# A hybrid encoder block on one core: a wider in-projection chunk, a tap on another engine, a regrouped filter chain and regrouped attention products

## The chip, the cores and the metric

The kernel runs on one core of a Trainium2 chip. The metric is the device time of one execution in microseconds (us); of several runs the median counts. TensorE does the matrix products (PE in the rows; PEld is its loading of weights), VectorE (DVE) and ScalarE (ACT) the elementwise work, GpSimd (POOL) the rest of it, and SP issues most of the transfers.

## The reference

Inputs are x (1, 2048, 1024) in f32, p, and the weights of one layer. What matters here:

```python
h = rms_norm(x, g_mix);  proj = h @ w_in           # w_in: 1024 x 2304
q, k, v, u = proj[:512], proj[512:640], proj[640:768], proj[768:]   # last axis
ya = attention_group(q, k, v, q_gain, k_gain)      # 8 query heads, 2 kv heads, 64 each
yh = hyena_group(u, conv_w, conv_b, ...)           # 3 x 512 channels
x = x + concat(group_rms(ya), group_rms(yh)) @ w_out
x = x + hierarchical_moe(rms_norm(x))              # 32 experts, top 2 of one group
x = x + (p @ w_ple) * sigmoid(rms_norm(x) @ w_ple_gate + b)
return rms_norm(x)
# hyena_group: uc = conv_b + sum_j shift(u, j) * conv_w[j]  (3 taps), split into v, x1, x2
#   y = x2 * conv(h2, x1 * conv(h1, v)); the filters h1, h2 (2048 long, two-sided) come from
#   a small sine network times a decay, divided by the sum of their absolute values, by FFT
```

## The kernel before

The program is written as Python generators that emit instructions; a framework sets semaphores, assigns buffers from pools and orders each engine's queue when the program is built, earlier emitted work first where it can go. `block_kernel` (L1787) runs two generators side by side with `interleave` (L91): each yields the planned cost of what it has just emitted, and the one that is behind its share goes next.

The left side is `stage_in` (L104) and then `Attention.run` (L749). `stage_in` takes the tokens in four quarters of 512. A quarter normalises and transposes its x (L157 to L178) into a high and a low part, `xh` and `xl`. Then come three chunks of 256 columns of `w_in` for q, k and v (`tokens`, L181): a weight chunk is loaded (L133), split into high and low (`split_w`, L136: ScalarE copies the high part, GpSimd or VectorE subtracts), and `product` (L145) makes 24 matmuls for each of four token tiles, into one of three PSUM banks (`in_pm`, L114); ScalarE copies the result out (L187) and one store for each chunk sends it to `qkv_d`. Then twelve tiles of 128 channels for the Hyena inputs (`channels`, L192): a product with 512 tokens, a copy into `U` (L204), the three-tap convolution with the middle tap on VectorE (L209) and the two others after it (L212), four transposes back to token order (L219), a copy and stores to `uc_d`. In the last quarter the attention's pools open (L236), its first preparation (`begin`) is emitted between the channel tiles, and `K.uc_done` tells the right side which third of `uc_d` is complete.

The right side is `stage_filter` (L319), `stage_hyena` (L482), and part of the per-layer embedding (`Ple.run`, L1501). The filter stage makes a small sine network's output `h2`, and then takes eight pairs of order and channel block: `gen` (L384) in eight turns makes a product (L394), multiplies by the decay into `g` (L401, eight buffers, `GB`) and adds up absolute values (L402); `norm` (L407) sums (L411 to L422, each product through the one bank of `fi_p`), scales `g` (L435) and corrects one row (L437); `fft1` (L440) makes eight products (L444, the same bank), copied out by ScalarE (L446) and stored; `fft2` (L450) follows one pair later. L467 to L479 emit `gen` of one pair, `fft1` of the pair before and `fft2` of the one before that in turn. `stage_hyena` transforms `uc_d` blocks, multiplies with the filters and transforms back; L541 is the gating after its last product.

`Attention.run` goes through 16 units (8 heads, two halves of the queries). For each of 16 key tiles a unit makes four score products (L798, L801) into two `ps` banks, two exponentials on ScalarE (L802), and two value products (L811), which lag two key tiles behind (`PV_LAG`); GpSimd and VectorE add up the exponentials (L821). Each step also emits up to two steps of the next unit's preparation (L733, L735). `K.behind` keeps score and value products in order. The banks:

```python
banks = {"pa": [(psa, "pa")] * 3, "ps": [(pss, "ps")] * 2}
for j, (h, u) in enumerate(self.order):
    wait -= K.banks_free                 # set when the right side has emitted its last
    if wait == -BANKS_AFTER:             # BANKS_AFTER = 2
        psx = self.pool("at_px", 1, space=PSUM)
        for tag in banks:
            banks[tag].append((psx, tag))
```

After both sides come the output projection, the experts and the tail, which the change leaves alone.

Of the kernel before, what the change touches and what calls it, by code (L numbers as in the profile page):

```python
# [8 lines left out]
F32 = mybir.dt.float32  # L9
# [27 lines left out]
GB = 8  # L37
# [5 lines left out]
PV_LAG = 2  # L43
# [60 lines left out]
def stage_in(K, st, x, g_mix, w_in, conv_w, conv_b, qkv_d, uc_d, pa, attn):  # L104
# [9 lines left out]
    pst, psm = pool("in_pt", 2, s_ps, space=PSUM), pool("in_pm", 3, s_ps, space=PSUM)  # L114
# [6 lines left out]
    K.uc_done, K.banks_free = 0, False  # L121
# [9 lines left out]
    def load_w(c0, n, pool, tag):  # L131
        raw = pool.tile([P, 8, n], F32, tag=tag, name="raw")
        nc.sync.dma_start(raw, w_in[:, c0:c0 + n].rearrange("(k p) n -> p k n", p=P))  # L133
        return raw

    def split_w(raw, n, pool, tags, on_pool, bufs=2):  # L136
        wh, wl = [pool.tile([P, 8, n], F32R, tag=tag, name=nm, bufs=bufs) for tag, nm in zip(tags, ("wh", "wl"))]
# [5 lines left out]
        return wh, wl  # L143

# [7 lines left out]
    for h in range(NQ):  # L152
        last, first = h == NQ - 1, h > 0
        xh, xl = [[pa.tile([P, 4, HT], F32R, tag=f"{nm}{q}", name=nm) for q in range(2)] for nm in ("xh", "xl")]
        cols = [2, 0, 1] if last else [0, 1, 2]
        raws = []
        for t in range(HTT):  # L157
# [5 lines left out]
            if t < 2:  # L163
                raws.append(load_w(cols[t] * 256, 256, praw, "raw"))
# [16 lines left out]
        def tokens(c, wh, wl):  # L181

            stg = pa.tile([P, HTT, 256], F32, tag="stg", name="stg", bufs=2)
            for t in range(HTT):
                ps = psm.tile([P, 512], F32, tag="pm", name="ps")
                product(ps[:, :256], lambda k: xs(k, slice(t * P, (t + 1) * P)), lambda k: (wh[:, k], wl[:, k]))
                nc.scalar.copy(stg[:, t], ps[:, :256])  # L187
                yield 2.6
            nc.sync.dma_start(qkv_d[h * HT:(h + 1) * HT, c * 256:(c + 1) * 256]
                              .rearrange("(t p) n -> p t n", p=P), stg)  # L190

        def channels(ct, stg, wh, wl):  # L192
# [10 lines left out]
            product(ps, lambda k: (wh(k), wl(k)), lambda k: xs(k, slice(None)))  # L203
            nc.scalar.copy(U[:, o0:o0 + HT], ps)  # L204
            if not last:
# [3 lines left out]
            nc.vector.tensor_scalar(out=acc[:, :n_out], in0=U[:, 1:1 + n_out], scalar1=wcol(1),  # L209
                                    scalar2=wcol(3), op0=ALU.mult, op1=ALU.add)  # L210
# [3 lines left out]
            if first:  # L214
                nc.gpsimd.tensor_copy(fix[:, h - 1, ct:ct + 1], acc[:, 0:1])
            pt = pst.tile([P, 512], F32, tag="pt", name="pt")
            for k in range(HTT):
                t0 = o0 - 1 + k * P
# [8 lines left out]
        for c in cols:  # L227
            raw = raws.pop(0) if raws else load_w(c * 256, 256, praw, "raw")
            if h == 0 and c == 0:
                consts()  # L230
            yield from tokens(c, *split_w(raw, 256, pw, ("wh", "wl"), not (c == 2 or (h == 0 and c < 2))))
        if last:
            while not K.filter_done:
                yield 0.05
            s_e.close()
            pb = attn.open(lambda tag: pst.tile([P, 512], F32, tag="pt", name=tag))  # L236
            ahead = attn.begin()
            raws = [load_w(768 + i * P, P, pb, "raw") for i in range(2)]
        for ct in range(12):
            part, cs = ct // 4, slice(ct // 2 % 2 * 256, (ct // 2 % 2 + 1) * 256)  # L240
            if last:
                raw = raws.pop(0)
                w4 = split_w(raw, P, pb, ("w", "w"), ct % 3 != 2, 4)
                if ct < 10:
                    raws.append(load_w(768 + (ct + 2) * P, P, pb, "raw"))
                wh, wl = [lambda k, w=w: w[:, k] for w in w4]
            else:
                if ct % 2 == 0:
                    raw = load_w(768 + ct * P, 256, praw, "raw")
                    w4 = split_w(raw, 256, pw, ("wh", "wl"), ct % 6 != 4)  # L250
                wh, wl = [lambda k, w=w: w[:, k, ct % 2 * P:(ct % 2 + 1) * P] for w in w4]
# [1645 lines left out]
```

## Time and profile before

| | |
|---|---|
| median of 3 runs | 3165.42 us (3157.89 to 3170.35) |
| profiled execution, its own time | 3178.87 us |
| its span, first to last instruction | 3177.1 us |
| TensorE busy | 2905.4 us (91%) |
| VectorE, ScalarE, GpSimd busy | 2047.3, 1322.0, 1143.2 us |
| mean granted TensorE clock | 0.951 of full |
| instructions | 50424 |

Busy time is a sum over stages with different limits, so a view by stretch says more than the whole. A wait in a row is idle time of the engine named first, put down to what came last. An instruction's line is the line of the kernel that made it; one made by a helper carries the helper's line (L74, L80, L88). Matmuls overlap, so the distance from start to start tells their cost better than their duration.

### The profile page before, as it was taken

How to read it: one execution, taken by the hardware profiler on the slowest of the kernel's cores; microseconds unless marked ns; L12 is line 12 of the kernel's file. 1: busy time of each engine (PE TensorE's matmuls, PEld its weight loads, DVE VectorE, ACT ScalarE, POOL GpSimd, SP SyncE). 2: the span in 40 equal slices, each digit the busy share in tenths (PEclk: the TensorE clock that was granted, in tenths of full speed). 3: DMA queues.
4: the chain of work that ended last, by engine and by line, in shares of the span. 5: the costliest groups of instructions: out<-in, count | busy, mean ns of one | idle time of the engine just before them, and what ended most of it. 6: DMA issues, size and time to landing. Idle time of an engine off the chain costs nothing. (4 is left out here: it accounts for less than half of the span.)

```text
span 3177.1 us, 50424 instructions
## 1 busy us (share of the span) xinstructions
PE 2905.4 (91%) x19001; PEld 1937.3 (61%) x19001; DVE 2047.3 (64%) x2737; ACT 1322.0 (42%) x1975; POOL 1143.2 (36%) x1058
## 2 busy tenths in 40 slices
PE   7989889798899999759999999989999999998897
PEld 5757667575445453524444488856667777675776
DVE  5865656536677776628887745366667677675665
ACT  3232233332344434225444422245556566664332
POOL 1423323242355555218877643011111211121443
PEclk9989889898999999879999999989999999999999
DMA  6477787786755765651000254379789888897553
GB/s 196 146 219 245 212 251 238 225 262 187 222 164 171 204 179 168 177 170 44 18 12 15 65 168 140 137 230 337 249 274 340 292 305 284 309 322 250 180 180 112
DMA packets 471989, 627.45 MB, mean 197 GB/s; under 512 B 64597, under 2 KB 302984, under 8 KB 467262
## 3 DMA queue, kind: packets, MB, share of 16 engines
q1 hardware_dynamic: 451630, 568.73, 55.7%
q0 software_dynamic: 20112, 55.47, 5.5%
q8 instruction: 150, 2.46, 0.3%
q14 instruction: 97, 0.79, 0.1%
HBM read 462.45 MB, written 161.56 MB: 196 GB/s over the span
## 5 line engine op out<-in xcount | busy, mean ns | idle before, releaser
L1306 DVE TENSOR_TENSOR wl<-raw,wh 128x1024 fp32r<-128x1024 f32 x384 | 462.8, 1223 | 202.2 <-ACT wh L1301 192.8
L1301 ACT CAST wh<-raw 128x1024 fp32r<-128x1024 f32 x384 | 398.2, 1051 | 262.9 <-PE ps L1324 87.5
L821 POOL TENSOR_TENSOR sums<-e,sums 128x512 f32<-128x512 f32 x306 | 412.4, 1364 | 145.9 <-ACT e L802 135.7
L802 ACT ACTIVATE e<-ps 128x512 f32<-128x512 f32 x512 | 290.1, 596 | 330.8 <-PE ps L801 278.5
L735 DVE TENSOR_REDUCE mx<-pa 128x1 f32<-128x512 f32 x512 | 330.1, 683 | 100.9 <-PE pa L733 100.2
L811 PE MATMUL po<-e,v 128*64 128x512 f32 x1024 | 290.0, 624 | 0.0
L1401 POOL DMA_DIRECT2D y_d<-ob x64 | 36.0, 564 | 556.8 <-DVE ob L1400 349.4
L1322 PE MATMUL ps<-wh,xt 128*128 128x512 f32 (+4 forms) x512 | 212.8, 416 | 9.5 <-ACT wh L1301 9.3
L1323 PE MATMUL ps<-wl,xt 128*128 128x512 f32 (+4 forms) x512 | 207.5, 405 | 7.1 <-DVE wl L1306 7.1
L1324 PE MATMUL ps<-wh,xt 128*128 128x512 f32 (+4 forms) x512 | 203.6, 398 | 0.0
L148 PE MATMUL ps<-xh,wh 128*128 128x512 f32 x384 | 157.7, 411 | 8.1 <-ACT U L204 8.1
L733 PE MATMUL pa<-kst,q 128*128 128x512 f32 x352 | 140.3, 450 | 22.6 <-DVE mx L735 20.2
L149 PE MATMUL ps<-xl,wh 128*128 128x512 f32 x384 | 159.3, 415 | 0.0
L150 PE MATMUL ps<-xh,wl 128*128 128x512 f32 x384 | 158.0, 411 | 0.4 <-POOL wl L88 0.4
L88 POOL TENSOR_TENSOR wl<-raw,wh 128x2048 fp32r<-128x2048 f32 (+1 forms) x26 | 102.8, 3956 | 150.3 <-ACT wh L138 144.8
L798 PE MATMUL ps<-q,kst 128*128 128x512 f32 x352 | 151.5, 431 | 3.6 <-ACT e L802 3.6
L801 PE MATMUL ps<-q,k 65*128 65x512 f32 x352 | 141.9, 403 | 4.7 <-DMA q<-mr 4.7
L821 DVE TENSOR_TENSOR sums<-e,sums 128x512 f32<-128x512 f32 x110 | 120.5, 1102 | 34.7 <-ACT e L802 34.0
L733 PEld LDWEIGHTS pa<-kst,q 128*128 128x128 f32 x352 | 63.3, 191 | 123.1 <-DVE mx L735 73.0
L1271 POOL DMA_INDIRECT g<-h_d,idx x52 | 74.5, 1433 | 165.5 <-PE pt L1289 66.4
L148 PE MATMUL ps<-wh,xh 128*128 128x256 f32 x384 | 121.6, 317 | 4.7 <-ACT xh L79 2.4
L1322 PEld LDWEIGHTS ps<-wh,xt 128*128 128x128 f32 (+4 forms) x512 | 96.0, 188 | 47.0 <-ACT wh L1301 13.7
(370 smaller groups left out, 6631.5 us busy)
## 6 DMA issues: line engine op xcount, KB each, us to landing
raw<-in_w_gate_dram SPq DMA_DIRECT2D x128, 512.0 KB
raw<-in_w_up_dram SPq DMA_DIRECT2D x128, 512.0 KB
raw<-in_w_down_dram SPq DMA_DIRECT2D x128, 512.0 KB
h_f<-hs SPq DMA_DIRECT2D x256, 128.0 KB
ab<-h_f SPq DMA_DIRECT2D x32, 1024.0 KB
raw<-in_w_in_dram SPq DMA_DIRECT2D x30, 1024.0 KB
xt<-in_x_dram SPq DMA_DIRECT2D x32, 512.0 KB
dec<-in_c_decay_dram SPq DMA_DIRECT2D x64, 256.0 KB
```

Source lines behind the costliest of these rows:

```text
L148: nc.tensor.matmul(ps, lh, rh, start=(k == 0), stop=False)
L149: nc.tensor.matmul(ps, lh, rl, start=False, stop=False)
L733: nc.tensor.matmul(pa, qh[:, t * P:(t + 1) * P], self.kst[g][:, q * 512:(q + 1) * 512], start=True, stop=True)
L735: nc.vector.tensor_reduce(out=mx[:, t, q:q + 1], in_=pa, axis=AX.X, op=ALU.max)
L802: nc.scalar.activation(out=pe[:, i], in_=ps, func=AF.Exp, scale=0.125)
L811: mm = nc.tensor.matmul(po[H2[i]], v[:, kt, g * 64:(g + 1) * 64], pe[:, i], start=(kt == 0), stop=(kt == NT - 1), skip_group_check=True)
L821: acc[j][1].tensor_tensor(out=sums[j], in0=pe[:, i], in1=src, op=ALU.add)
L1301: nc.scalar.copy(hi, raw)
L1306: nc.vector.tensor_tensor(out=lo, in0=raw, in1=hi.bitcast(F32), op=ALU.subtract)
L1322: nc.tensor.matmul(ps[:m], xt[:, k, 0, :m], hv[:, j], start=(k == 0), stop=False)
L1323: nc.tensor.matmul(ps[:m], xt[:, k, 0, :m], lv[:, j], start=False, stop=False)
L1324: nc.tensor.matmul(ps[:m], xt[:, k, 1, :m], hv[:, j], start=False, stop=(k == 7))
```

## The change

The chunks of the in-projection's q, k, v part become 384 columns wide (two for three) and those of the channels 384 too (four for six); each is loaded and split in two halves of 512 rows. Products get two PSUM banks for three. The token results leave in a store for each tile, from buffers of `U` and `acc`. The convolution's middle tap goes to ScalarE. A channel tile's transposes are emitted after the next tile's product (in the last quarter at the latest after every fourth). The filters' small bank becomes two, `GB` goes from 8 to 10, and the first transform's turns begin two turns later. Hyena's pools open only after the in-projection's are closed (`K.room`). In the attention two key tiles' value products are emitted together, four in a row, and the sums of a key tile directly after its exponentials.

```diff
-GB = 8
+WC = 384
+GB = 10
-PV_LAG = 2
+PV_AT = 2
-    pst, psm = pool("in_pt", 2, s_ps, space=PSUM), pool("in_pm", 3, s_ps, space=PSUM)
+    pst, psm = pool("in_pt", 2, s_ps, space=PSUM), pool("in_pm", 2, s_ps, space=PSUM)
...
+    def chunk(c, raws=()):
+        parts = []
+        for i in range(2):
+            raw = raws[i] if raws else load_part(c, i)
+            n_piece[0] += 1
+            parts.append(split_w(raw, pw, ("wh", "wl"), n_piece[0] > 4 and n_piece[0] % 3 != 0, (4, 3)))
+        return lambda k, cols: [w[:, k % 4, cols] for w in parts[k // 4]]
...
-        def tokens(c, wh, wl):
-            stg = pa.tile([P, HTT, 256], F32, tag="stg", name="stg", bufs=2)
+        def tokens(c, w):
             for t in range(HTT):
                 ps = psm.tile([P, 512], F32, tag="pm", name="ps")
-                product(ps[:, :256], ...)
-                nc.scalar.copy(stg[:, t], ps[:, :256])
-                yield 2.6
-            nc.sync.dma_start(qkv_d[h * HT:(h + 1) * HT, c * 256:(c + 1) * 256]..., stg)
+                product(ps[:, :WC], ...)
+                so = pa.tile([P, HT + 4], F32, tag=("U", "acc")[t % 2], name="so", bufs=2)[:, :WC]
+                nc.scalar.copy(so, ps[:, :WC])
+                nc.sync.dma_start(qkv_d[h * HT + t * P:..., c * WC:(c + 1) * WC], so)
+                yield 4.3
...
-            nc.vector.tensor_scalar(out=acc[:, :n_out], in0=U[:, 1:1 + n_out], scalar1=wcol(1),
-                                    scalar2=wcol(3), op0=ALU.mult, op1=ALU.add)
+            nc.scalar.activation(out=acc[:, :n_out], in_=U[:, 1:1 + n_out], func=AF.Identity, scale=wcol(1),
+                                 bias=wcol(3))
...
+        def convolved():
+            late = None
+            for ct in range(12):
...
+                made = (ct, *channels(ct, w))
+                yield 5.6
+                if late is not None:
+                    yield late
+                late = made
+                if last and ct % 4 == 3:
+                    yield late
+                    late = None
...
-    pc, psm, psd = pool("fi_c", 1), pool("fi_p", 1, space=PSUM), pool("fi_d", 1, space=PSUM)
+    pc, psm, psd = pool("fi_c", 1), pool("fi_p", 2, space=PSUM), pool("fi_d", 1, space=PSUM)
...
-        for _ in range(8):
+        for i in range(8):
             for p in parts:
-                yield next(p, 0.0)
+                if p is not one or i >= GB - 8:
+                    yield next(p, 0.0)
...
+            for kt in range(NT):
+                scores(kt)
+                add_up(*late[-1])
+                if kt % PV_AT == PV_AT - 1 and kt >= 2 * PV_AT - 1:
+                    values(late[:PV_AT])
+                    del late[:PV_AT]
+                yield
+            values(late)
...
             K.filter_done = True
+            while not K.room:
+                yield 0.05
```

## Rows read from the trace of the kernel before

**Rows 1.** Busy time by stretch: TensorE, weight loads, VectorE, ScalarE, GpSimd, clock, DMA.

```profile
core 0: us, PE busy (x) PEld busy (x) DVE busy (x) ACT busy (x) POOL busy (x), PEclk, DMA share, GB/s
0.00:667.00 667.00, 577.50 (x4576) 446.02 (x4577) 404.17 (x476) 216.03 (x321) 201.89 (x226) 0.92 0.72 220
830.00:1300.00 470.00, 451.00 (x3374) 220.62 (x3373) 332.00 (x465) 192.55 (x319) 256.72 (x207) 0.97 0.62 180
1416.00:1818.00 402.00, 394.02 (x1514) 179.41 (x1517) 316.83 (x428) 193.62 (x345) 318.68 (x229) 1.00 0.12 34
```

**Rows 2.** Timeline, 1300 to 1420 us: start, duration, engine, line, tiles [idle before].

```profile
1300.22 0.40 PE L801 MATMUL ps<-ql,k 65*128 65x512 f32 x1
...
1389.77 0.69 DVE L541 TENSOR_TENSOR z<-ph,gt 128x512 f32<-128x512 f32 x1 [3.13 <-PE ph L539]
...
1415.39 0.39 PE L1531 MATMUL pp<-plh,pl 128*128 128x512 f32 x1
...
1418.26 1.28 POOL L821 TENSOR_TENSOR sums<-e 128x512 f32<-128x512 f32 x1 [107.30 <-ACT e L802]
```

**Rows 3.** Timeline, products of 256 and of 512 columns, a store's issue.

```profile
664.84 0.43 SPq L189 DMA_DIRECT2D qkv_d<-stg  x1
...
665.10 0.28 PE L148 MATMUL ps<-wh,xh 128*128 128x256 f32 x1
...
665.22 0.28 PE L149 MATMUL ps<-wl,xh 128*128 128x256 f32 x1
...
668.65 0.40 PE L148 MATMUL ps<-xh,wh 128*128 128x512 f32 x1
...
668.88 0.39 PE L149 MATMUL ps<-xl,wh 128*128 128x512 f32 x1
```

**Rows 4.** What TensorE waited for, 0 to 667 us: total, times, longest.

```profile
PE ps L444 <- DVE g L437: 19.6, 7, 6.1
PE ps L444 <- ACT sg L446: 13.5, 7, 3.8
...
PE pt L219 <- DVE acc L212: 9.4, 7, 2.9
...
PE ps L418 <- DVE acc L411: 8.3, 4, 3.4
...
PE ps L413 <- ACT sg L446: 4.7, 4, 3.3
```

**Rows 5.** The taps by line (min/median/max ns), and two timeline rows at 315 us.

```profile
L209 DVE TENSOR_SCALAR acc<-U,cw x48: 528/544/4655, 85.7 to 803.5; 128x513 f32<-128x513 f32 x36, 128x512 f32<-128x512 f32 x12
...
L212 DVE SCALAR_TENSOR_TENSOR acc<-U,cw,acc x96: 656/754/4822, 86.8 to 805.5; 128x513 f32<-128x513 f32 x72, 128x512 f32<-128x512 f32 x24
...
314.93 4.60 POOL L88 TENSOR_TENSOR wl<-raw,wh 128x2048 fp32r<-128x2048 f32 x1
...
315.16 4.66 DVE L209 TENSOR_SCALAR acc<-U,cw 128x513 f32<-128x513 f32 x1
```

**Rows 6.** ScalarE: the sine's durations (ns), and its wait for weight buffers, 0 to 667.

```profile
L363 ACT ACTIVATE h<-sa x8: 617/633/637, 28.2 to 93.8; 128x512 f32<-128x512 f32 x8
...
ACT wh L138 <- PE ps L149: 56.1, 16, 6.7
```

**Rows 7.** What TensorE waited for, 667 to 830 us.

```profile
PE ps L148 <- ACT U L204: 8.1, 2, 4.1
```

**Rows 8.** Timeline of TensorE, 1285 to 1295 us: one pair of value products, then two.

```profile
1285.69 0.39 PE L801 MATMUL ps<-q,k 65*128 65x512 f32 x1
1286.01 1.08 PE L811 MATMUL po<-e,v 128*64 128x512 f32 x4
1287.02 0.97 PE L733 MATMUL pa<-kst,q 128*128 128x512 f32 x3
...
1293.15 1.94 PE L811 MATMUL po<-e,v 128*64 128x512 f32 x8
1295.01 0.73 PE L733 MATMUL pa<-kst,q 128*128 128x512 f32 x2
```

More of the change, by code (lines that the diff above doesn't have):

```diff
@@ L120, in stage_in @@
     gB = pc.tile([P, D], F32, name="gB")
-    K.uc_done, K.banks_free = 0, False
+    K.uc_done, K.banks_free, K.room = 0, False, False
     def consts():
@@ L227, in stage_in @@
         for c in cols:
-            raw = raws.pop(0) if raws else load_w(c * 256, 256, praw, "raw")
+            w = chunk(c, raws)
+            raws = ()
             if h == 0 and c == 0:
                 consts()
-            yield from tokens(c, *split_w(raw, 256, pw, ("wh", "wl"), not (c == 2 or (h == 0 and c < 2))))
+            yield from tokens(c, w)
         if last:
@@ new lines, in convolved @@
+        def convolved():
+            late = None
+            for ct in range(12):
+                if last:
+                    w2 = split_w(raws.pop(0), pb, ("w", "w"), ct % 3 != 2, (4, 4))
+                    if ct < 10:
+                        raws.append(load_w(768 + (ct + 2) * P, P, pb))
+                    w = lambda k: [a[:, k] for a in w2]
+                else:
+                    if ct % 3 == 0:
+                        w3 = chunk(2 + ct // 3)
+                    w = lambda k: w3(k, slice(ct % 3 * P, (ct % 3 + 1) * P))
+                made = (ct, *channels(ct, w))
[6 more added lines that the diff above has]
+                    late = None
+            if late is not None:
+                yield late
@@ L252, in stage_in @@
+        for step in convolved():
+            if isinstance(step, float):
+                yield step
+                if last:
+                    for _ in range(2):
+                        if next(ahead, "end") != "end":
+                            yield 0.44
+                continue
+            ct, acc, o0 = step
+            part, cs = ct // 4, slice(ct // 2 % 2 * 256, (ct // 2 % 2 + 1) * 256)
             if ct % 2 == 0:
                 stg = pa.tile([P, HTT, 256], F32, tag="stg", name="stg", bufs=2)
-            channels(ct, stg, wh, wl)
@@ L255, in stage_in @@
-            yield 5.6
-            if last:
-                for _ in range(2):
-                    if next(ahead, "end") != "end":
-                        yield 0.44
+            token_major(ct, acc, o0, stg)
             if ct % 2 == 0:
@@ new lines, in scores @@
+            def scores(kt):
+                nonlocal last
+                pe = pb.tile([P, 2, 512], F32, tag="w", name="e", bufs=4)
+                ks = slice(kt * P, (kt + 1) * P)
+                for i in range(2):
+                    ps = bank("ps")
+                    mm = nc.tensor.matmul(ps, self.kst[g][:, ks], qh[:, ql_s[i]], start=True, stop=False)
+                    if last is not None:
+                        K.behind(mm, last)
+                    last = nc.tensor.matmul(ps, self.k1[g][:, ks], ql[:65, ql_s[i]], start=False, stop=True)
+                    nc.scalar.activation(out=pe[:, i], in_=ps, func=AF.Exp, scale=0.125)
+                late.append((kt, pe))
@@ new lines, in values, with add_up @@
+            def values(tiles):
+                nonlocal last
+                with K.tc.high_priority():
+                    for kt, pe in tiles:
+                        for i in range(2):
+                            mm = nc.tensor.matmul(po[H2[i]], v[:, kt, g * 64:(g + 1) * 64], pe[:, i],
+                                                  start=(kt == 0), stop=(kt == NT - 1), skip_group_check=True)
+                            K.behind(mm, last)
+                            last = mm
+            def add_up(kt, pe):
```

69 lines of the change are left out of this document (20 added, 49 removed).

## The prediction

> **What bounds the kernel now.** I read the busy time by stretch first. In 0 to 667 us the in-projection (left side) and the filters' chain (right side) share TensorE: it is busy 577.5 of 667 us at a granted clock of 0.92, a mix of its two levels (1.2 and 2.4 GHz) [rows 1]. VectorE is busy 404, ScalarE 216, so TensorE is what the stretch is made of, and its idle 89.5 us is the most that better overlap can give there. From 667 to 830 the last quarter's channels run beside the attention's first preparation and the first steps of the Hyena stage. From 830 to 1300 attention units and Hyena steps share TensorE (451 of 470 us). From 1416 to 1818 attention is alone and TensorE is busy 394 of 402 us at full clock, GpSimd 319, VectorE 317, ScalarE 194 [rows 1].
>
> Between them lies a hole. At 1300.22 the attention's first step of a new unit has issued its scores; the next exponentials reach GpSimd only at 1418.26, after 107.3 us without one [rows 2]. In between run the rest of the Hyena stage (last gating at 1389.77) and the per-layer-embedding products, whose last one starts at 1415.39. The kernel says why: `run` adds a third score bank at the start of the unit at which `wait` is -BANKS_AFTER, and that bank is one that the right side gives back only when its last product is out. So 830 to 1416 is as long as the right side, whatever the attention does, and a gain in the units before the hole counts only as far as it also moves Hyena.
>
> **The in-projection by 384 columns.** A 256-column product starts every 0.12 us (665.10, 665.22), a 512-column one every 0.23 (668.65, 668.88) [rows 3]. The tokens' part has 4 quarters x 3 chunks x 4 tiles x 24 = 1152 of the first, 138 us; it gets 4 x 2 x 4 x 24 = 768 of 384 columns. Not shown; not under 0.12 (92 us) and not over 0.23 (179 us), so -46 to +41. Cost grows by 0.11 for 256 more columns, so I take halfway, 0.176: 135 us, -3, and at the clock of that stretch **-4 us**. Weights are the same bytes, in 52 loads for 42; tokens leave in 32 stores for 12. The 30 more issues cost SP 0.43 us each [rows 3], 13 us on a queue that has the whole stretch; I put them at 0, since loads are asked for a chunk ahead; without that cover, +13.
>
> **The filters' chain.** TensorE waits for it by name [rows 4]: 19.6 us for the correction that ends a normalisation (L437), 13.5 for ScalarE to empty the one bank (L446), 8.3 for the sum over parts (L411), 4.7 again for the bank before the norm's first product (L413): 46.1 us. A second bank goes at the 13.5 and 4.7; ten buffers for `g` and a first transform that starts two turns later let the next order's first two products and decays run while a normalisation ends, which goes at the 19.6 and 8.3. What is late next is the in-projection's own product in front of each filter step (24 of them, 5.6 us): order on TensorE is fixed when the program is built. So I take half, **-23 us**, with ends 0 and -46. Products that no longer stop also lift the clock a little: **-5 us** (0 to -20; at 0.92 the mean loses 53 us to the lower level).
>
> **The tap on ScalarE, and transposes one channel tile later.** VectorE loses 48 instructions of 0.544 us in the median but up to 4.66: the one at 315.16 lies under GpSimd's 4.60 us subtraction at 314.93 and ends with it [rows 5]. ScalarE gains 48 Identity activations; nearest row: the sine over 128x512, 0.633 us [rows 6], so 30 us, beside TensorE, on an engine busy a third of the time; without that cover, +30. TensorE waits 9.4 us for the taps before the transposes [rows 4]; with the late transposes I take **-7 us** (-9 to 0).
> What VectorE loses to GpSimd need not vanish: the next instruction on the same tile, L212, reads two SBUF inputs and shows a maximum of 4.82 us [rows 5]. The Trainium skill (SBUF — State Buffer, Who interferes with whom) says that VectorE, in a two-port mode or with two SBUF inputs, and GpSimd exclude each other for a whole instruction; by that rule the trace agrees, the wait passes on to L212, and this term would be -3 instead of -7. The Trainium skill (ScalarE: Activation LUTs, What ACT_TABLE_LOAD costs) prices an activation with two pointer operands at 0.186 + 2 x 0.093 + 513 x 0.000833 = 0.80 us, an estimate; ScalarE would then gain 38 us, and the sum would be the same.
>
> **Two banks for products instead of three.** The bank given to the filters comes from here. An eviction must now end within one product. Today products wait for an eviction 8.1 us in the last quarter [rows 7] and next to nothing before. I take **+10 us**; ends 0 and +65, below. Behind a waiting product stand all later ones and the filters' steps, since TensorE is one queue.
>
> **Values' products in fours.** A pair of products lies between a score product at 1285.69 and the next one at 1287.02: 0.32 + 1.01 us; two pairs in a row take 1293.15 to 1295.01, 1.86 [rows 8]. Of the 0.32, 0.23 is the score product's own. Apart, 2 x (0.09 + 1.01) = 2.20; together 0.09 + 1.86 = 1.95: 0.25 us for each merger. A unit has 14 runs now (the last three pairs already touch) and 7 after: 1.75 us. Nine units lie behind the hole: **-16 us**. The seven before it save 12 us of TensorE in the stretch that Hyena shares; Hyena is also held by its own chain, so I take half, **-6 us** (0 to -12). The sums move ahead of the products and free their buffers earlier; GpSimd is busy 319 of 402 us [rows 1], so at nothing.
>
> **Where the hole stays.** Adding the planner's yields by hand: the embedding part ends at 623.7 of its scale before, between the starts of units 5 (608.4) and 6 (645.5); after, 636.5 between 621.2 and 658.3, since Hyena waits for `uc_done` either way. So unit 7 asks for the bank as before; waiting for `room` adds nothing.
>
> **Sum.** -4 -23 -5 -7 +10 -16 -6 = -51 us. The profiled execution took 3178.9 us (span 3177.1), which gives 3128; the median of the runs is 13.5 lower, so 3114 us. A difference of 0.5% (16 us) is about what a measurement of this kernel can tell from none.
>
> **Rivals.** *The chain opens wholly*: all 46.1 us and the 20 us of clock go; 38 us more: 3076. For it: four changes at one chain. Against: products of the in-projection still stand between its steps. *TensorE was full anyway*: the filters' waits fill with other waits, the terms -23, -5 and -7 go and the +10 with them: 3165 - 26 = 3139. For it: TensorE is busy 87% of that stretch. *Scores run dry*: four score pairs in a row need two or three banks emptied at about 0.6 us each; half a us for each of 7 runs in 16 units is 56 us, less what preparation products fill; with half of that left, 3142. Against: three banks behind the hole. *Two banks hold up the products* (the other side): ScalarE stands 56.1 us in 16 waits, 6.7 at the longest, before a weight cast whose buffer a product still reads [rows 6]. With three banks nobody needed it then; with two, an eviction queued behind makes TensorE wait as long, and the 30 us of taps stand in the same queue. There are 32 + 48 = 80 products; the other terms sum to -61, so at 0.76 us a product nothing is left, and at 56 + 30 = 86 us the time is 3190. *The regrouping does not appear*: the order could split the fours again; -22 falls away, 3136, inside the second case.
>
> **Chances.** Forecast 0.45; chain wholly open 0.15; TensorE full 0.17; scores dry 0.08; two banks 0.15. Faster by over 0.5% (under 3149.6): 0.45 + 0.15 + 0.13 of the third + 0.02 of the fourth = 0.75. Slower (over 3181.2): most of the last, 0.13. Within: 0.12. The range reaches below the open chain and up to where the two banks begin to cost more than all gains: 3068 to 3178, leaving out some 0.06 below and 0.12 above. Of the cases with a gain alone it would be 3076 to 3142.
>
> **What would show it.** Right: TensorE's waits for L437, L446 and L411 in the first stretch under 25 us in sum; the hole's end some 35 us before 1418; runs of eight value records, and some 1.75 us less for each unit behind the hole; a hole that still ends with the last embedding product. Wrong: TensorE waiting for copies of `U` or `so` by more than 40 us; units behind the hole no shorter; an activation-table load at each tap; or the hole longer by what the stretch before gained.

## The result, and the profile after

The changed kernel takes 3196.8 us in the median of 7 executions (3189.6 to 3202.4); the kernel before 3168.7 us beside it (3157.9 to 3176.1). The ratio is 1.0092, 95% interval 1.0077 to 1.0107: **slower by 28 us**, where 3114 us were forecast.

The kernel before varies by itself. The execution behind the rows ahead of the prediction took 3178.9 us; a second traced one, in the run e18, took 3157.7 us. Their instructions agree, the waits named in [rows 4] differ by a few us (the filters' four sum to 46.1 us in the first and 39.2 in the second), and the hole ends at 1418 us in one and at 1393 in the other. The changed kernel's traced execution (3195.2 us) lies near its median. So stages are compared with the second trace, whose time lies 11 us under the median of its kernel, and a difference of some 10 us between two traces is not read as an effect.

Busy time by stage, the second trace of the kernel before (columns as in [rows 1]; the cuts are the end of the last quarter's tokens, of its channels, of unit 6, of the hole, and of the attention):

```profile
0.00:657.00 657.00, 569.97 (x4582) 440.72 (x4583) 402.24 (x478) 216.55 (x323) 200.38 (x226) 0.93 0.74 224
657.00:786.00 129.00, 111.84 (x698) 79.11 (x696) 82.14 (x119) 41.15 (x62) 42.11 (x54) 0.93 0.68 211
786.00:1280.00 494.00, 465.58 (x3727) 232.31 (x3727) 348.19 (x489) 202.80 (x337) 259.43 (x211) 0.98 0.64 188
1280.00:1393.00 113.00, 61.09 (x647) 35.38 (x646) 36.47 (x51) 14.89 (x21) 1.64 (x1) 0.71 0.62 176
1393.00:1793.00 400.00, 392.09 (x1505) 177.93 (x1505) 314.05 (x427) 192.98 (x343) 318.44 (x229) 1.00 0.12 33
1793.00:3156.00 1363.00, 1288.04 (x7851) 958.85 (x7851) 857.57 (x1178) 654.42 (x891) 319.30 (x337) 0.97 0.70 240
```

The same stages of the changed kernel:

```profile
0.00:680.00 680.00, 576.04 (x4198) 439.84 (x4199) 375.52 (x446) 241.64 (x352) 200.50 (x230) 0.91 0.72 219
680.00:823.00 143.00, 115.08 (x726) 79.69 (x724) 77.43 (x109) 48.09 (x72) 40.45 (x55) 0.88 0.60 186
823.00:1310.00 487.00, 455.09 (x3692) 237.14 (x3692) 347.07 (x489) 204.39 (x340) 260.97 (x212) 0.98 0.64 190
1310.00:1428.00 118.00, 62.19 (x650) 35.06 (x649) 34.56 (x49) 14.39 (x20) 1.65 (x1) 0.68 0.56 164
1428.00:1830.00 402.00, 384.50 (x1512) 192.16 (x1512) 310.76 (x427) 191.46 (x344) 324.42 (x229) 0.97 0.12 34
1830.00:3193.00 1363.00, 1287.34 (x7847) 955.49 (x7843) 857.64 (x1178) 654.97 (x890) 316.98 (x337) 0.98 0.70 240
```

The first two stages are longer by 23 and 14 us, the units before the hole shorter by 7, the hole longer by 5, the units behind it by 2, the rest equal: 37 us between these two traces. Up to the hole's end TensorE is busy 1208 us in both; idle are 185 us before and 220 after. Of these 35 us more, 28 lie in the first two stages, with the in-projection and the filters.

Equal busy time is not equal work, since part of it runs at the lower clock level. Counted at the granted clock (each moment of busy time times the share of the clock granted then), TensorE's work over the whole span is 2798 us in both traces of the kernel before and 2763 us in the changed kernel. So the change does save 36 us of work. Against that stand 45 us more of idle time and 27 us more of busy time lost to the lower level. Two traces of the kernel before differ by 4 us in the one and by 17 in the other, so the idle time is clear of that spread and the clock's part is so only in part.

What TensorE waited for up to 690 us in the changed kernel (total, times, longest), against [rows 4]:

```profile
PE pt L238 <- DVE acc L228: 23.1, 8, 6.5
PE ps L482 <- DVE g L475: 16.8, 6, 7.6
PE ps L482 <- ACT sg L484: 13.9, 7, 4.3
...
PE ps L451 <- ACT sg L484: 5.6, 2, 3.3
...
PE ps L456 <- DVE acc L449: 3.9, 2, 3.1
```

The filters' four waits sum to 40.2 us; they were 46.1 in the first trace of the kernel before and 39.2 in the second, so hardly anything of them went. The channels' transposes wait 23.1 us for the taps, where they waited 9.4 and 6.7. In five of these eight waits, 14.5 us, VectorE had itself stood idle for the tap on ScalarE; in the longest the tap stands behind a weight cast that waited 8.4 us for its load.

In the second stage, SyncE's queue. The first load of Hyena follows the store of the last quarter's first pair of channel tiles:

```profile
727.00 0.37 SPq L306 DMA_DIRECT2D uc_d<-stg  x1
729.87 2.64 SPq L547 DMA_DIRECT2D z<-uc_d  x4
```

In the kernel before, the two went out at 691.9 and 697.1 us in the first trace, and in the second at

```profile
679.15 0.51 SPq L268 DMA_DIRECT2D uc_d<-stg  x1
...
684.21 2.62 SPq L507 DMA_DIRECT2D z<-uc_d  x4
```

which is 22 us after the last quarter's tokens ended; here it is 47 us after. The taps of that pair were done by 698 us after the change too; its transposes stand on TensorE at 718 us, behind two more products and the attention's preparation.

Behind the hole the fours are there, TensorE at 1524 us:

```profile
1524.73 1.94 PE L853 MATMUL po<-e,v 128*64 128x512 f32 x8
1526.59 0.50 PE L839 MATMUL ps<-q,kst 128*128 128x512 f32 x1
```

TensorE is busy 7.6 us less there and idle 9.6 us more. Its work at the granted clock is 17.6 us less (372.8 for 390.4): 10 us of the saving go to the lower clock level, 9.6 to idle time. One gap, 1681 to 1686, and the granted clock after it, by 5 us:

```profile
1676.00:1681.00 5.00, 5.00 (x22) 2.63 (x21) 3.64 (x6) 2.19 (x5) 4.92 (x5) 1.00 0.17 57
1681.00:1686.00 5.00, 1.49 (x8) 0.66 (x6) 4.86 (x5) 0.89 (x2) 4.92 (x4) 1.00 0.24 54
1686.00:1691.00 5.00, 5.00 (x16) 2.08 (x16) 3.67 (x6) 1.02 (x2) 2.07 (x2) 0.66 0.00 0
1691.00:1696.00 5.00, 5.00 (x22) 2.81 (x21) 4.21 (x7) 2.31 (x5) 4.23 (x3) 1.00 0.01 2
```

VectorE is full (4.86 of 5 us) while TensorE stands: a preparation product waits 3.5 us for a row maximum.

### The profile page after: what moved, and what is told of

Same layout as the page of the kernel before. It is cut to its first block, busy times and chain, and to the rows that moved or that the text cites. A ratio compares the mean times of both kernels' runs of the same rounds, so it can differ in the third digit from the quotient of the medians.

```text
span 3193.4 us, 49755 instructions
## 1 busy us (share of the span) xinstructions
PE 2880.2 (90%) x18617; PEld 1939.4 (61%) x18617; DVE 2003.0 (63%) x2693; ACT 1354.9 (42%) x2017; POOL 1145.0 (36%) x1064
## 4 chain that ended last, share of the span: by engine, by line
PE 52%; DMA 11%; DVE 7%; issue 4%; ACT 2%; POOL 2%; SPq 1%; DVEq 0%; POOLq 0%; ACTq 0%
PE po L853 6%; PE ps L1373 4%; PE ps L1374 4%; PE ps L1375 4%; PE pr L1379 3%; PE pa L773 3%; PE ps L839 3%; PE ps L842 2%; PE ps L1439 2%; PE ps L1441 2%; PE ps L1440 2%; PE pr L1446 2%; PE ps L1012 2%; PE ps L1013 2%; PE ph L345 2%
## 5 line engine op out<-in xcount | busy, mean ns | idle before, releaser
L865 POOL TENSOR_TENSOR sums<-e,sums 128x512 f32<-128x512 f32 x306 | 420.3, 1392 | 132.2 <-ACT e L843 128.4
L853 PE MATMUL po<-e,v 128*64 128x512 f32 x1024 | 274.0, 630 | 0.0
L228 DVE SCALAR_TENSOR_TENSOR acc<-U,cw,acc 128x513 f32<-128x513 f32 (+1 forms) x96 | 94.5, 989 | 127.3 <-ACT acc L225 120.8
L773 PE MATMUL pa<-kst,q 128*128 128x512 f32 x352 | 139.1, 445 | 25.6 <-DVE mx L775 16.6
L853 PEld LDWEIGHTS po<-e,v 128*64 128x64 f32 x1024 | 67.8, 141 | 133.6 <-issue 126.5
L140 ACT CAST wh<-raw 128x1536 fp32r<-128x1536 f32 (+1 forms) x52 | 71.7, 1378 | 166.8 <-DMA raw<-in_w_in_dram 129.3
L89 POOL TENSOR_TENSOR wl<-raw,wh 128x1536 fp32r<-128x1536 f32 (+1 forms) x32 | 106.9, 3344 | 79.2 <-issue 33.1
L1379 PE MATMUL pr<-raw,xr 128*32 128x128 f32 (+1 forms) x2112 | 126.2, 303 | 0.4 <-DVE ob L1455 0.4
```

What stands on the lines that cost most here:

```text
L773: nc.tensor.matmul(pa, qh[:, t * P:(t + 1) * P], self.kst[g][:, q * 512:(q + 1) * 512], start=True, stop=True)
L853: mm = nc.tensor.matmul(po[H2[i]], v[:, kt, g * 64:(g + 1) * 64], pe[:, i], start=(kt == 0), stop=(kt == NT - 1), skip_group_check=True)
L865: acc[j][1].tensor_tensor(out=sums[j], in0=pe[:, i], in1=src, op=ALU.add)
L1379: nc.tensor.matmul(pr[c * R:(c + 1) * R, mi * n2:(mi + 1) * n2], xr[:, k, :R], raw[:, j, c * n2:(c + 1) * n2], start=(mi == 0 and k == 0), ...
```

## The experiments

Ratios are to the kernel before, run beside each, with 95% intervals; the changed kernel stands at 1.0092 (1.0077 to 1.0107).

### One part of the change undone

**e1**, tap back on VectorE:

```diff
-            nc.scalar.activation(out=acc[:, :n_out], in_=U[:, 1:1 + n_out], func=AF.Identity, scale=wcol(1),
-                                 bias=wcol(3))
+            nc.vector.tensor_scalar(out=acc[:, :n_out], in0=U[:, 1:1 + n_out], scalar1=wcol(1),
+                                    scalar2=wcol(3), op0=ALU.mult, op1=ALU.add)
```

> The changed kernel with the middle tap back on VectorE, the rest as changed. Theory 1 (the tap now stands in ScalarE's queue behind weight casts and stores that wait for transfers, so the accumulators and TensorE's transposes come late: its idle time ahead of the transposes went from 9.4 to 23.1 us up to the end of the tokens of the last quarter): that idle time falls to 10 us or less, the first stage ends some 14 us earlier (667 in place of 681 us) and the time is 3183 us, 0.4% under the changed kernel. Theory 2 (the filters' chain now runs ahead of the in-projection, which then stands alone at the end with gaps that nothing fills; the tap is not the cause): the stage ends at 678 to 682 us and the time is 3193 to 3199 us.

Measured: 3193.5 us, 1.0074 (1.0050 to 1.0097). The wait before the transposes is 16.4 us, between the theories' figures; idle time up to the tokens' end 110 us for 104. Undoing the tap does not take the stage's idle time away; a gain of a few us can't be told from none.

**e2**, values in pairs, sums behind them, as before:

```diff
-            for kt in range(NT):
-                scores(kt)
-                add_up(*late[-1])
+            for kt in range(NT + PV_LAG):
...
```

> The changed kernel with the values' products and the sums in the order of the kernel before (pairs, two key tiles late). Theory A (the fours save 9 us of TensorE in the units behind the hole, and preparation products that wait for VectorE's maxima give 10 us back): the units behind the hole take as long as in the changed kernel within 4 us, TensorE's idle time there falls from 17.5 to some 8 us, and the time is 3193 to 3201 us. Rival (the fours bring what I forecast, and the loss is all elsewhere): 13 to 22 us slower than the changed kernel, 3210 to 3219 us.

Measured: 3191.5 us, 1.0083 (1.0061 to 1.0104). Behind the hole TensorE is busy 395 us and idle 13 of 408, where the fours have 384 and 18 of 402: they save 10 us of busy time there and give 4 back as idle time. The time excludes the rival's 3210 us. Theory A is nearer, but its own figures (within 4 us of 402, some 8 us idle) are missed by a little.

**e3**, the filters' chain as before, and **e17**, only the bank given back:

```diff
-    pst, psm = pool("in_pt", 2, s_ps, space=PSUM), pool("in_pm", 2, s_ps, space=PSUM)
+    pst, psm = pool("in_pt", 2, s_ps, space=PSUM), pool("in_pm", 3, s_ps, space=PSUM)
...
-    pc, psm, psd = pool("fi_c", 1), pool("fi_p", 2, space=PSUM), pool("fi_d", 1, space=PSUM)
+    pc, psm, psd = pool("fi_c", 1), pool("fi_p", 1, space=PSUM), pool("fi_d", 1, space=PSUM)
```

and in e3 also

```diff
-GB = 10
+GB = 8
...
-                if p is not one or i >= GB - 8:
-                    yield next(p, 0.0)
+                yield next(p, 0.0)
```

> The changed kernel with the filters' chain of the kernel before: one product bank for the filters and three for the in-projection, eight buffers for g, first step not later. Theory 1 (tap): TensorE's idle time ahead of the transposes stays near 23 us; what the chain brought is lost as well, so 3197 to 3210 us. Theory 2 (filters ahead, in-projection behind): the filters end near 655 us again, the stage ends at 667 to 672 us, and the time is 3183 to 3188 us.

> The changed kernel with one product bank for the filters and three for the in-projection, all else as changed (ten buffers, later first step, tap, late transposes, fours). If the bank costs here what it costs the kernel before (+32 us alone, +23 with the second bank given to the filters): 3165 to 3177 us. If the cost of a part depends on what stands around it (undoing the whole chain gave 7 us): 3185 to 3197 us.

Measured: e3 3187.0 us, 1.0070 (1.0048 to 1.0092). The time is in theory 2's range, the stages are not: the tokens end at 649 us and the filters only at 693, later than in either kernel, and the interval reaches the changed kernel's. e17 3191.0 us, 1.0098 (1.0082 to 1.0114): in the changed kernel, moving a bank from the products to the filters costs nothing that shows, as the second of its cases said.

**e5**, transposes at once in all quarters, **e6**, in the last quarter alone:

```diff
                 made = (ct, *channels(ct, w))
+                if last:
+                    yield made
+                    yield 5.6
+                    continue
                 yield 5.6
```

(this is e6; e5 does it without the condition)

> The changed kernel with each channel tile's transposes right behind its taps again, in all quarters, the rest as changed. Theory 3 (the transposes of the last quarter's first pair of channel tiles, which the first Hyena load needs, run at 718 us although their accumulators were ready before 698, behind two later products and the attention's preparation; the first Hyena load goes out at 730 us in place of 697): the first pair's transposes run by 700 us, Hyena's first forward step 15 to 25 us earlier than 738, the hole ends at 1408 to 1415 in place of 1428 us, and the time is 3177 to 3186 us. Rival (Hyena's start has slack; what bounds the hole is TensorE's sum of work): hole's end within 5 us of 1428, time 3192 to 3200 us.

> The changed kernel with the transposes put right behind the taps in the last quarter alone; the first three quarters keep them one channel tile late. Theory 3: the same gain as with all quarters or a few us more, as the first three quarters lose nothing: hole's end 1405 to 1415, time 3172 to 3186 us. Rival: within 5 us of the changed kernel, 3192 to 3200 us.

Measured: e6 3182.2 us, 1.0045 (1.0028 to 1.0061), 15 us under the changed kernel with no overlap of the intervals. SyncE in e6:

```profile
698.72 0.38 SPq L307 DMA_DIRECT2D uc_d<-stg  x1
...
703.57 2.63 SPq L548 DMA_DIRECT2D z<-uc_d  x4
```

and its second stage:

```profile
680.00:801.00 121.00, 109.71 (x727) 76.96 (x725) 76.90 (x108) 49.46 (x73) 41.28 (x56) 0.96 0.71 221
```

22 us less for that stage, 28 us less for the store, and the hole ends at 1413 for 1428. Theory 3 is shown for the last quarter. e5 gives 3193.5 us, 1.0077 (1.0060 to 1.0094): its second stage is as short (120 us), but the transposes of the first three quarters wait 31.9 us and the hole ends at 1423. So the delay harms in the last quarter; that it helps in the first three is likely, but the two intervals touch (1.0060 and 1.0061).

### Parts on the kernel before

**e4** is values in fours (the edit of e2 reversed); **e9** the whole chain (e3 reversed); **e16** the tap (e1 reversed). **e7** is the changed kernel with the edits of e1, e2, e3 and e5 together, so the in-projection by 384 columns alone; **e8** the same without the edit of e2. **e13** has two product banks and leaves the third unused:

```diff
-    pst, psm = pool("in_pt", 2, s_ps, space=PSUM), pool("in_pm", 3, s_ps, space=PSUM)
+    pst, psm = pool("in_pt", 2, s_ps, space=PSUM), pool("in_pm", 2, s_ps, space=PSUM)
```

**e14** adds the filters' second bank:

```diff
-    pc, psm, psd = pool("fi_c", 1), pool("fi_p", 1, space=PSUM), pool("fi_d", 1, space=PSUM)
+    pc, psm, psd = pool("fi_c", 1), pool("fi_p", 2, space=PSUM), pool("fi_d", 1, space=PSUM)
```

**e15** on the kernel before, and **e10** on e8, have the buffers and the later step:

```diff
-GB = 8
+GB = 10
...
-                yield next(p, 0.0)
+                if p is not one or i >= GB - 8:
+                    yield next(p, 0.0)
```

> The kernel before with the values' products in fours and the sums moved ahead, nothing else. Theory A (given back at the preparation products): within 5 us of the kernel before, 3164 to 3172 us; the nine units behind the hole take 355 to 360 us. Rival (the forecast's term): 16 to 22 us faster, 3147 to 3153 us, 1.75 us less for each unit behind the hole.

> Of the change only the in-projection by 384 columns (with its two loads a chunk and its token tiles stored one by one) and the wait for room: tap on VectorE, transposes at once, filters' chain, three product banks and values' products as in the kernel before. Theory 4 (the in-projection part is harmless, my forecast -4; the loss is in the other parts): 3160 to 3169 us, the tokens of the last quarter end at 645 to 660 us. Rival (the in-projection's own part, more loads behind one another on one queue with two raw buffers and later weight casts, makes the loss): 3180 us or more, tokens of the last quarter at 668 us or later.

> The same as the in-projection alone, and the values' products in fours with the sums ahead. Theory A (given back at preparation products that wait for VectorE): within 5 us of the in-projection alone. If the fours gain 6 us before the hole as the fours alone showed (hole's end 1410.9 for 1417.6): 6 to 8 us below it, 3153 to 3162 us, and then below the kernel before.

> The kernel before with the filters' chain of the change alone: two product banks for the filters and two for the in-projection, ten buffers for g, first step two turns later. My forecast's terms for it (-23 for the chain, -5 for the clock, +10 for the bank taken from the in-projection): 3145 to 3155 us, TensorE idle some 25 us less up to the end of the last quarter's tokens. Theory 2 (the filters only run earlier and push the in-projection back, which then stands alone at the end; idle time is moved, not removed): the filters end 40 us or more before the tokens, the tokens of the last quarter end later than 668 us, idle time up to there 85 us or more, and the time is 3168 to 3185 us.

> In-projection by 384 columns and values in fours, as in the run of that name, and of the filters' chain the ten buffers for g and the later first step, but one product bank for the filters and three for the in-projection. If the buffers and the later step shorten the filters' chain by themselves: the filters end before 690 us (700.6 without them), Hyena's first step 10 us earlier than 722, hole's end at 1395 to 1403 (1407.6), 3160 to 3168 us. If the second bank was what moved the filters: filters' end within 5 us of 700, hole's end and time as without, 3170 to 3176 us.

> The kernel before with two product banks for the in-projection in place of three; the bank is left unused. My forecast's term: +10 us (ends 0 and +65), 3177 us, with TensorE waiting for copies of U or of the tokens by some 10 us more. If two are enough: 3164 to 3171 us.

> The kernel before with two product banks for the filters and two for the in-projection, eight buffers for g and the first step where it was. Forecast: the waits for the one bank (13.5 and 4.7 us) go, some -18 +10: 3159 us. Theory 2 (waits move to the channels' transposes, since TensorE's order lets the filters go first): TensorE's wait for the taps before the transposes at 25 us or more (9.4 before), filters' end before 620 us, 3175 to 3195 us.

> The kernel before with ten buffers for g and the filters' first step two turns later, one bank for the filters and three for the in-projection. Forecast: the waits for the correction and the sum (19.6 and 8.3 us) go by half, -14: 3154 us. By the run that added them to the in-projection by 384 columns: filters' end 20 to 35 us earlier than 661, the channels of the last quarter later, 3176 to 3190 us.

> The kernel before with the middle tap on ScalarE, nothing else. Forecast: -4 to -7 us with the transposes at once, 3160 to 3164 us. Theory 1: ScalarE's queue delays the taps behind weight casts and evictions, TensorE's wait before the transposes goes from 9.4 to 20 us or more, 3172 to 3180 us. Within 3 us of 3168: the two cancel.

Measured, with the ends of filters, tokens and hole and the idle time up to the tokens' end by the trace:

| run | us | ratio (interval) | filters, tokens, hole end | idle |
|---|---|---|---|---|
| before, second trace | 3157.7 | | 650, 657, 1393 | 87 |
| e4 fours | 3171.6 | 1.0016 (1.0001 to 1.0031) | 662, 669, 1411 | 96 |
| e7 384 columns | 3189.1 | 1.0057 (1.0039 to 1.0076) | 690, 638, 1403 | 84 |
| e8 384 columns, fours | 3173.3 | 1.0012 (0.9998 to 1.0026) | 701, 647, 1408 | 92 |
| e9 chain | 3198.6 | 1.0106 (1.0087 to 1.0125) | 587, 670, 1414 | 106 |
| e10 e8, GB 10, later step | 3189.2 | 1.0078 (1.0060 to 1.0096) | 666, 650, 1413 | 88 |
| e13 two product banks | 3201.4 | 1.0099 (1.0082 to 1.0115) | 657, 664, 1420 | 93 |
| e14 e13, two filter banks | 3192.4 | 1.0069 (1.0053 to 1.0085) | 617, 678, 1419 | 105 |
| e15 GB 10, later step | 3181.4 | 1.0042 (1.0025 to 1.0058) | 627, 659, 1404 | 91 |
| e16 tap | 3184.3 | 1.0039 (1.0023 to 1.0054) | 644, 661, 1423 | 92 |
| changed kernel | 3196.8 | 1.0092 (1.0077 to 1.0107) | 612, 680, 1428 | 104 |

No part alone makes the kernel before faster. e4 has theory A's time, though its nine units behind the hole take 398 us and not the 355 to 360 that I had expected. e9 and e14 end the filters early as theory 2 said; e9 is 14 us slower than its range, and in e14 the wait for the taps is 19.3 us, under the 25 expected, while the wait for the normalised x is 32.0. e15 keeps to the slower of its cases; e16 is 4 us slower than its own, and its wait before the transposes did not rise. e13 is over my term's 10 us and under its end. e7 has the rival's time though its tokens end early, and e8 takes 16 us less than e7 where at most 8 were expected. e10 fits neither of its cases: the filters end 35 us earlier than in e8, as the first said, and the time is 16 us longer. Why is not known. The parts do not add up: chain, fours, tap and columns alone are 1.06 + 0.16 + 0.39 + 0.57 = 2.18% slower, the change 0.92%; a bank moved from the products to the filters costs 23 us in e14 and nothing that shows in e17.

**e9 settles the largest term.** TensorE's waits in e9, up to 690 us:

```profile
PE pt L219 <- DVE acc L212: 37.3, 13, 13.0
PE ps L444 <- ACT sg L446: 21.6, 7, 7.3
PE pt L175 <- DVE xn L170: 20.9, 7, 8.9
...
PE ps L444 <- DVE g L437: 3.7, 4, 1.8
...
PE ps L413 <- ACT sg L446: 1.8, 1, 1.8
...
PE ps L418 <- DVE acc L411: 1.4, 2, 1.1
```

The filters' four waits fall from 46.1 [rows 4] (39.2 in the second trace) to 28.5 us, and the transposes' wait for the taps rises from 9.4 to 37.3, that for the normalised x (L170) from 8.6 to 20.9. In twelve of the thirteen waits for the taps, 24 us, VectorE is busy nearly throughout, with the filters' work and with taps held up by GpSimd (one takes 4.77 us beside a subtraction of 4.94); between 100 and 200 us it is busy 90 us in e9 and 83 before. The longest, 13.0 us, is of another kind. VectorE stands idle too, until a store has landed and its copy can have the buffer:

```profile
620.25 0.69 DVE L225 COPY stg<-pt 128x512 f32<-128x512 f32 x1 [13.40 <-DMA uc_d<-stg]
```

The filters end 74 us earlier than in the first trace of before, and the in-projection then stands alone for 83 us with 16 idle, of which this wait is 13.

Not all four waits fell. Those for the correction (L437) and the sum (L411) went from 27.9 to 5.1 us, those for ScalarE's evictions (L446) from 18.2 to 23.4. In the kernel before, the eviction is often itself waiting for a store, which stands behind others in SyncE's queue:

```profile
412.54 7.52 SPq L463 DMA_DIRECT2D h_f<-hs  x8
420.16 0.38 SPq L447 DMA_DIRECT2D s_f<-sg  x1
...
424.03 0.59 ACT L446 COPY sg<-ps 128x512 f32<-128x512 f32 x1 [6.15 <-DMA s_f<-sg]
...
424.76 2.05 PE L444 MATMUL ps<-g,w 128*128 128x512 f32 x2 [3.75 <-ACT sg L446]
```

So it is in seven of the eleven waits there, 15.2 of the 18.2 us, and in all twelve of e14, where the second bank leaves these waits at 18.4 us:

```profile
PE ps L444 <- ACT sg L446: 14.9, 9, 4.0
...
PE ps L413 <- ACT sg L446: 3.5, 3, 2.1
```

What holds the product up in these waits is the buffer `sg`, not the bank. In e15, with the ten buffers and the later step and one bank, the four waits sum to 11.6 us, and the taps (25.9 us) and the loads of `zt` (25.0) are waited for instead.

Up to the filters' end TensorE is idle 86 to 98 us in all these kernels, whether that end lies at 587 or 701 us: the waits change partners.

**e16 settles the tap.** VectorE's next taps in e16 (count, busy, mean, idle before):

```profile
L212 DVE SCALAR_TENSOR_TENSOR acc<-U,cw,acc 128x513 f32<-128x513 f32 (+1 forms) x96 | 106.1, 1109 | 59.1 <-ACT acc L209 56.1
```

That line was busy 80.5 us before, so 25.6 us passed on to it. The moved line had been busy 56.0 us, 48 x 0.544 = 26.1 of it its own work [rows 5]; of the 29.9 above that nearly all stays on VectorE. By the rule cited in the prediction (the Trainium skill, SBUF — State Buffer, Who interferes with whom) the trace agrees. The wait before the transposes did not reach the 20 us that theory 1 wanted, it fell to 4.4 us; what rose is the filters' wait for the evictions (L446), 33.6 us for 18.2. In 29.6 of these ScalarE was waiting for a store of `sg` as above, so it is not the tap that they stand behind. Why the tap alone costs 12 us is therefore not shown. The tap's own 0.817 us on ScalarE is near the estimate from the Trainium skill (ScalarE: Activation LUTs, What ACT_TABLE_LOAD costs), 0.80, not the sine's 0.633.

**e13 stays partly open.** Beside the second trace of before it is longer by 7 us to the tokens' end, 11 in the last quarter's channels, 16 in the units up to the hole and 8 behind it. Its work at the granted clock is hardly different (2793 for 2798 us); beside that trace 25 us more are idle and 20 more go to the lower level. One piece can be named, in the last unit, where the sums' product waits 4.7 us for GpSimd:

```profile
PE pa L833 <- POOL sums L821: 4.7, 1, 4.7
```

after which the granted clock falls:

```profile
1788.00:1793.00 5.00, 2.65 (x10) 0.89 (x11) 1.87 (x4) 1.22 (x2) 5.00 (x4) 0.62 0.00 0
1793.00:1798.00 5.00, 5.00 (x13) 2.25 (x11) 3.83 (x3) 2.39 (x4) 4.65 (x4) 0.50 0.07 7
1798.00:1803.00 5.00, 5.00 (x17) 2.25 (x18) 3.27 (x8) 2.28 (x4) 2.93 (x3) 0.85 0.00 0
```

From its first exponential to its last the last unit takes 43 us there, 36 in both traces of before; e9, e14, e15 and e16 show the same (41 to 43). No bank stands in that row. TensorE's waits for evictions of the two banks are 7.7 us in the last quarter (8.1 in [rows 7]). That the instructions stand in another order is what I suspect; it was not tried by itself. e7 takes 1378 us behind the attention, with unchanged code there, where the others take 1356 to 1370: its work there is the same 1268 us, and 32 us of busy time go to the lower clock level where the others lose 15 to 26.

### The hole

**e11**, e8 with the third score bank asked for one unit later; **e12**, the kernel before with the fours and the same:

```diff
-BANKS_AFTER = 2
+BANKS_AFTER = 3
```

> In-projection by 384 columns and values in fours, and the third score bank asked for one unit later (at the ninth unit in place of the eighth), nothing else. Theory 5 (what the first stage gains is swallowed by the hole: the attention's units before it end 21 us earlier than in the kernel before, and the eighth still waits for the last embedding product, with TensorE idle 60 us): the eighth unit runs in the hole with two banks, TensorE's idle time from the seventh unit's end to the last embedding product falls by 20 to 40 us, the attention ends at 1775 to 1790 in place of 1808 us, the time is 3140 to 3160 us. Rival (the eighth unit in the hole delays Hyena by as much as it gains): hole's end or last embedding product 20 us or more later, time 3168 to 3180 us.

> The kernel before with values in fours and the third score bank asked for one unit later. Theory 5: the eighth unit runs in the hole; with 118 us of hole, 53 of them idle on TensorE, 15 to 30 us less than the fours alone: 3142 to 3157 us. Rival: Hyena is held up by as much, 3168 to 3178 us.

Measured: **e11 3140.1 us, 0.9911 (0.9895 to 0.9928)**, 27 us under the kernel before; e12 3156.2 us, 0.9965 (0.9951 to 0.9979). The hole in e11, from unit 6's end on:

```profile
1268.00:1412.00 144.00, 105.63 (x1007) 57.38 (x1000) 72.19 (x106) 36.28 (x60) 36.52 (x28) 0.83 0.60 173
1412.00:1772.00 360.00, 338.35 (x1337) 168.65 (x1337) 274.31 (x373) 170.92 (x308) 288.72 (x202) 0.98 0.13 35
```

Unit 7 now runs inside it (it ends at 1333 us), TensorE is idle 38 us of 144 where e8 had 60 of 130, and the hole's end has hardly moved, 1412 us (1408 in e8). Theory 5 is shown. A gain ahead of the hole was swallowed before: e7 ends unit 6 at 1260 us, against 1300 and 1280 in the two traces of before, and its hole is 143 us long, against 118 and 113. (e8, 1278 and 130, is clear of the first trace alone.) The four runs together say the same: with the bank asked for as before, the columns bring nothing (e8 1.0012, e4 1.0016); with it asked for later they bring 17 us (e11 0.9911, e12 0.9965).

**e18**, the kernel before once more:

> The kernel before, unchanged, for a second trace. Its time should lie at 3158 to 3176 us; I expect the hole's end at 1405 to 1418 us, the units behind it at 398 to 402 us and what lies behind the attention at 1350 to 1360 us.

Measured: 3157.7 us; the hole ends at 1393 us, earlier than I expected, the units behind it take 400 us, the rest 1363, 3 us over.

## Why the prediction was wrong

The change does save work on TensorE, 36 us at the granted clock; what I had wrong is what saved work and removed waits turn into. The sum's largest term failed, and measured alone it has the other sign. Term by term:

- **Chain, -23 us, and clock, -5**: wrong, in two steps. The first is "A second bank goes at the 13.5 and 4.7": 15.2 of these 18.2 us are evictions that wait for a store to free `sg`, and with the second bank 18.4 us remain (e14). The second is "What is late next is the in-projection's own product in front of each filter step". The buffers and the later step did take 23 us from the waits for the correction and the sum (e9); next came the channels' transposes, 37.3 us for 9.4, and the normalised x, 20.9 for 8.6. I had halved the gain for work on TensorE and looked neither at VectorE, busy 83 of 100 us in the stretch of a normalisation, nor at SyncE's stores. The whole part costs 31 us alone (e9), and the granted clock of the changed kernel's first stage is 0.91, for 0.92 and 0.93 in the two traces before.
- **Two banks for products, +10**: the range's upper end (+65) held the +32 of e13, but the mechanism (evictions that come late) does not show in its waits, and in the changed kernel giving the bank back gains nothing (e17). The rival that I had on the slower side, 3190 us, is near the time, and not by its reason.
- **Tap and late transposes, -7**: wrong. "TensorE waits 9.4 us for the taps before the transposes" was read for the first stage only. In the last quarter the delay moves a store that Hyena waits for by 28 us and costs 15 us (e6); I had not asked who waits for the transposes' result. The tap alone costs 12 us (e16): the wait on GpSimd passed on, as the rule said, so little could be gained; what makes it a loss stays open.
- **384 columns, -4**: a product starts every 0.174 us in the median, 0.176 was forecast. The cost of the products was right, and e7's work is 4.5 us less than before; alone the part is 0.57% slower all the same, with the fours 0.12%. What it saves before the hole the hole takes (e11).
- **Fours, -16 behind the hole and -6 before**: the runs of eight are there, and TensorE's work behind the hole falls by 17.6 us where 16 were forecast. The step that failed is to count saved work as saved time: 9.6 us more of gaps and 10 us more at the lower level (granted clock 0.97 for 1.00) gave it back, and the units take 402 us for 400. I had put the earlier sums "at nothing" and not named what else stands on VectorE.
- **What is shown of the 28 us, and what is not**: with tap, late transposes and chain undone together 25 us go (e8, 1.0012 for 1.0092). The late transposes of the last quarter are 15 of them (e6). The other parts, undone one by one, move the time, by their ratios, by 7 us or less (e1, e2, e3, e17), which can't be told from none; how the rest divides between the tap, the chain and the earlier transposes is open.
- **Right**: the hole still ends with the last embedding product (1427 us); no table load appears at the taps; the copies of `U` and `so` are waited for by 5.5 us, not 40.

## What to carry to other kernels

A wait named by the profile is removed only if the engine that ends it has time left and is not itself waiting: look one step further back (here an eviction that waited for a store's buffer, so that a second bank did not help), ask for each engine in the chain who else waits for it next, and count the idle time of the whole stretch rather than the wait's own row. When work is deferred, follow its result to the last reader: here a transposition nobody on its engine missed held up a load of the next stage. And where one late resource closes a stretch, as the score bank does here, move that first; gains ahead of it vanish until then.

## What the runs showed that I had not expected

- The same program's traced executions differ by 21 us (3157.7 and 3178.9), 24 of it before the hole's end, with 185 and 190 us idle there. The same work, 1142 us at the granted clock in both, took 1208 us in one and 1228 in the other: 67 and 86 us of it went to the lower clock level.
- Two gaps, of 3.5 and 4.7 us in full stretches, are followed by 5 to 10 us at a granted clock between 0.50 and 0.85. The one at 1681 us in the changed kernel costs (1 - 0.66) x 5 = 1.7 us more than its own length, the one in e13 (0.50 + 0.15) x 5 = 3.3 us behind its end.
- Kernels that differ in the first 700 us alone differ in the last attention unit 1100 us later: 36 us before, 41 to 43 in e9, e13, e14, e15 and e16. In each of the five the sums' product waits 3.6 to 5.3 us for GpSimd there; why GpSimd is late is not shown.
